# Gram products of an RWKV-7 chunk, parted by key tokens into quadrants

## The chip, the cores and the metric

The kernel runs on one core of a Trainium2 chip. The metric is the device time of the whole program in microseconds (us); lower is better. The core has five engines that run side by side: TensorE (PE in the profile, its weight loads PEld), VectorE (DVE), ScalarE (ACT), GpSimd (POOL) and SyncE (SP, which here issues nearly all DMAs).

## The reference, cut to what matters

One layer of a streaming encoder: RMSNorm, one input projection, two head groups, an output projection. The part that matters is the RWKV-7 recurrence of group A: 16 heads of width 64, in chunks of 64 tokens behind 16 meta tokens.

```python
CHUNK = 64; N_META = 16; SEQ = 512; RWKV_HEAD = 64; N_RWKV_HEADS = 16

def step(S, inp):
    r_t, w_t, k_t, v_t, kk_t, b_t = inp
    sa = jnp.einsum('bhvk,bhk->bhv', S, kk_t)
    S = (S * w_t[:, :, None, :]
         - sa[..., None] * b_t[:, :, None, :]
         + v_t[..., None] * k_t[:, :, None, :])
    y_t = jnp.einsum('bhvk,bhk->bhv', S, r_t)
    return S, y_t
...
hn = _rmsnorm(h_res, norm_in_g[l])
P = hn @ w_in[l]
...
y = _rwkv7_recurrence(rh, decay, kh, vh, kk, kk * ah)
...
bonus = jnp.sum(rh * kh * r_k[l], axis=-1, keepdims=True) * vh
y_a = (yn + bonus.reshape(bsz, L, D_RWKV)) * jax.nn.silu(g_r)
...
h_res = h_res + mix @ w_out[l]
```

The kernel computes a chunk at once instead of token by token. For that it needs, for each chunk and head, the products of two sets of 64 key vectors (b and k, scaled by the decays) with two sets of 64 token vectors (kk and r): a Gram matrix of 128 x 128. Only pairs with the key ahead of the token count, so each of its four 64 x 64 blocks is masked to a triangle.

## The kernel before, in words

The heads go in pairs, 8 in all; a pair fills the 128 partitions, one head on the first 64 and one on the last. The main work is the input projection: 65 column tiles of 128, each against all tokens with TensorE. A tile's weights come in four quarters. SyncE loads two quarters at a time (`wr`), ScalarE rounds a quarter (line 151), VectorE takes the remainder (line 152), and TensorE multiplies the rounded and the remaining parts (lines 352 and 367, `ps_k`, `ps_r`, `ps_v`, `ps_g`, `ps_C`, `ps_h`, `ps_B`, `ps_gc`).

The recurrence's preparation is threaded through this stream. `prepare(i)` handles a pair and calls `fill(ns)` wherever TensorE must not wait for the other engines: `fill` then issues main products worth that many nanoseconds. `until(...)` issues main products until a tile has been taken up. TensorE's order is the order in the program; the other engines' orders are planned from priorities (`ahead()` raises one) and a model of the engines. `later(ns, fn)` issues DMAs once so much main work has gone by, and `behind` issues one behind the last weight load.

The steps of `prepare(i)` that the change touches:

- `bk` holds per chunk the two key sets b and k and, for the second head, b once more (so that the order k, b can be read as one run); `ar` holds the two token sets. Lines 715, 718 and 726 fill `bk`.
- `gt` is the masked Gram tile, 128 rows (two key sets of 64) x 2 heads x 9 chunks x 128 (two token sets of 64); one buffer for even pairs, one for odd ones. Line 750 clears what the meta chunk leaves out.
- `gram` (line 754) issues, for each of 8 chunks and 2 heads, one fp32 product with 64 contracted rows, 128 keys as the stationary side and 128 tokens moving. Chunks 1 to 4 go to two banks `za` (the tag `tz`), chunks 5 to 8 to two banks `zc` (the tags `misc` and `ser`).
- `gram_meta` does the meta chunk and the key norms (line 786) in the next main tile's banks, ahead of the other chunks or behind them (`late`); line 775 masks, line 779 copies the norms.
- `masked` (line 795) multiplies a bank with the mask `gmask` into `gt`, one VectorE instruction for a head and four chunks.
- Lines 817 to 820 form the sums over a head for the bonus term in the bank with tag `ser` and copy them to `r`; line 917 multiplies them with v.
- Line 826 transposes the keys; line 841 stores `gt` (`sg`), line 849 reads it back as 16 x 16 blocks (`d`), lines 859 to 886 invert these on VectorE, line 901 stores the result and `load_inverse` brings it back.

`invert` then works on two pairs together: it builds the inverse of the 64 x 64 blocks from the 16 x 16 ones with small products (lines 961 to 1027). `recur` runs the chunks (lines 1100 to 1139), and the output projection follows (line 1381).

Of the kernel before, what the change touches and what calls it, by code (L numbers as in the profile page):

```python
# [9 lines left out]
F32 = mybir.dt.float32  # L10
# [79 lines left out]
def hymba_kernel(ctx: ExitStack, tc: tile.TileContext, xt, xtok, front, w_in, w_out, pv, lup, cst, msk, gf, out):  # L90
# [533 lines left out]
    def until(*key):  # L624
        while key not in ready:
            step()
# [22 lines left out]
    def c3(t):  # L649
        return t.rearrange("p (c s) -> p c s", s=CH)  # L650

    def lora_up(i):
# [40 lines left out]
    def prepare(i):  # L693
# [3 lines left out]
        ar = cq.tile([P, NCH, 2, CH], F32, tag="ar", name=f"ar{i}")  # L697
        bk = cq.tile([P, NCH, 3, CH], F32, tag="bk", name=f"bk{i}")
        e1 = cq.tile([P, NCH, CH + 1], F32, tag="e1", name=f"e1{i}")
# [15 lines left out]
        nc.vector.scalar_tensor_tensor(  # L715
            out=bk[:, :, 0], in0=c3(k), scalar=hv[:, 2, i : i + 1], in1=c3(te), op0=ALU.mult, op1=ALU.mult
        )
        nc.scalar.copy(bk[64:128, :, 2], bk[64:128, :, 0])
        nc.gpsimd.tensor_scalar(
# [5 lines left out]
        nc.vector.tensor_tensor(out=ta, in0=ta, in1=k, op=ALU.mult)  # L725
        nc.vector.tensor_tensor(out=bk[:, :, 1], in0=c3(ta), in1=c3(e2), op=ALU.mult)
        nc.gpsimd.tensor_copy(dd[:, :, place[i]], e1[:, :, CH])
# [22 lines left out]
        nc.gpsimd.memset(gt[:, :, 0, META:P], 0.0)  # L750

        def gram(z, c, c0):
            for h, hs, ho in heads:
                nc.tensor.matmul(  # L754
                    z[h][:, c - c0],
                    bk[hs, c, h : h + 2, :].rearrange("p a s -> p (a s)"),
                    ar[hs, c].rearrange("p a s -> p (a s)"),
                    start=True, stop=True,
                )

        def gram_meta():
            z = early or next_banks()
            norms = key_norms(z[0][:, 96 : 96 + NS])
            for h, hs, ho in heads:
                nc.tensor.matmul(
                    z[h][:, 0:META],
                    bk[hs, 0, h : h + 2, :].rearrange("p a s -> p (a s)"),
                    ar[hs, 0, 0, 0:META],
                    start=True, stop=True,
                )  # L770
            if p and "levels" in state:
                state["out"] = state.pop("levels").pop(0)(second_level(z))
            with ahead():
                for h in range(2):
                    nc.vector.tensor_tensor(
                        out=gt[:, h, 0, 0:META], in0=z[h][:, 0:META], in1=gmask[:, h, 0:META], op=ALU.mult
                    )
            with ahead():
                nc.scalar.copy(n2, norms)
            if "out" in state:  # L780
                state.pop("out")()
            state["banks"] = z
# [8 lines left out]

        def masked(z, c0, c1):
            with ahead():
                for h in range(2):
                    nc.vector.tensor_tensor(
                        out=gt[:, h, c0:c1],
                        in0=z[h],
                        in1=gmask[:, h].unsqueeze(1).to_broadcast([P, c1 - c0, P]),
                        op=ALU.mult,
                    )  # L800


# [16 lines left out]
        nc.tensor.matmul(zb, ones[:, 0:P], rl, start=False, stop=True)  # L819
        nc.scalar.copy(r, zb)  # L820
        fill(FW["misc"])


        bt = cq.tile([P, 2, NCH - 1, CH], F32, tag="bt", name=f"bt{i}")
        for a in range(2):
            nc.vector.transpose(bt[:, a], bk[:, 0 : NCH - 1, a])

# [76 lines left out]
        for h, hs, ho in heads:  # L904
            for b in range(2):
                for a in range(2):
# [757 lines left out]
```

## Time and profile before

| | |
|---|---|
| median of 3 runs | 993.47 us (991.86 to 994.09) |
| the profiled execution | 993.5 us, span 991.2 us |
| TensorE clock granted | 0.998 |
| busy: TensorE, its loads, VectorE, ScalarE, GpSimd | 99%, 92%, 71%, 39%, 13% |
| DMA | 176.89 MB, mean 178 GB/s |

The span runs from the first instruction to the last. A row of the profile names the line, the engine, the operation and the tiles (written <- read), then the shape; `x32` is the number of records. A form such as `64*128 64x128` at TensorE means 64 rows and 128 columns of the array in use, and 64 partitions x 128 elements moving. Each fp32 product here leaves two records. Matmul durations overlap in the pipeline; what a group costs is seen in the chain, where only the time that each adds is counted.

### The profile page before, as it was taken

The numbers are of one execution on the slowest core, as the hardware profiler recorded it, in microseconds if no ns is written. First come the engines' busy times: TensorE is split into PE (matmuls) and PEld (weight loads), VectorE is DVE, ScalarE is ACT, GpSimd is POOL, SyncE is SP. The second block draws the span as 40 slices with busy tenths as digits, with TensorE's granted clock in tenths as the row PEclk, the third lists the DMA queues.
The fourth block names the chain that finished last, engine by engine and source line by source line (L and its number), as shares of the span: only waits on it lengthen the run. The fifth ranks groups of instructions, "written<-read, shape, count | busy, mean of one in ns | idle before, by whom it ended". The sixth has DMA issues, their size and how long they took to land.

```text
span 991.2 us, 23393 instructions
## 1 busy us (share of the span) xinstructions
PE 981.2 (99%) x9511; PEld 907.4 (92%) x9511; DVE 707.8 (71%) x1413; ACT 390.4 (39%) x731; POOL 128.0 (13%) x242
## 2 busy tenths in 40 slices
PE   9999999999999999999999999999999999999996
PEld 8999999999998999998999998889889898788885
DVE  6777966578675679653779654465756697998897
ACT  7553432344322434322434323232332435546464
POOL 0110302012010121010111010011211102001001
PEclk9999999999999999999999999999999999999999
DMA  9526576246675385853375856988886697697654
GB/s 324 156 91 149 145 202 160 88 126 150 152 181 166 92 194 117 211 150 107 87 186 122 205 143 189 280 250 250 229 252 189 179 281 197 183 313 197 149 128 170
DMA packets 205387, 176.89 MB, mean 178 GB/s; under 512 B 138528, under 2 KB 168032, under 8 KB 204768
## 3 DMA queue, kind: packets, MB, share of 16 engines
q1 hardware_dynamic: 202688, 166.50, 60.2%
q0 software_dynamic: 2304, 8.39, 4.9%
q8 instruction: 74, 1.21, 0.5%
q10 hardware_dynamic: 288, 0.52, 0.1%
q14 instruction: 33, 0.27, 0.1%
HBM read 139.02 MB, written 36.35 MB: 177 GB/s over the span
## 4 chain that ended last, share of the span: by engine, by line
PE 94%; DVE 3%; DMA 1%; ACT 1%; issue 1%; SPq 0%; DVEq 0%; POOL 0%; ACTq 0%
PE ps_v L352 9%; PE ps_h L352 9%; PE ps_C L352 9%; PE ps_g L352 9%; PE ps_gc L367 9%; PE ps_B L367 9%; PE ps_k L352 8%; PE ps_r L352 8%; PE M L1381 5%; PE P L1381 4%; PE Q L1381 2%; PE g L754 2%; PE ps_lora L367 1%; PE ps_k L367 1%; PE zy L1139 1%; PE ps_r L367 1%
## 5 line engine op out<-in xcount | busy, mean ns | idle before, releaser
L151 ACT CAST w<-wr 128x512 fp32r<-128x512 f32 x252 | 153.7, 619 | 285.8 <-PE ps_C L352 47.5
L152 DVE TENSOR_TENSOR w<-wr,w 128x512 fp32r<-128x512 f32 x252 | 175.3, 707 | 117.7 <-ACT w L151 116.7
L352 PE MATMUL ps_v<-xh,w 128*128 128x256 f32 (+2 forms) x512 | 84.0, 285 | 0.0
L367 PE MATMUL ps_B<-xh,w 128*128 128x512 f32 x256 | 83.4, 394 | 0.0
L352 PE MATMUL ps_h<-xh,w 128*128 128x256 f32 (+2 forms) x512 | 81.6, 281 | 0.0
L352 PE MATMUL ps_g<-xh,w 128*128 128x256 f32 (+2 forms) x512 | 81.5, 281 | 0.0
L367 PE MATMUL ps_gc<-xh,w 128*128 128x512 f32 x256 | 81.1, 392 | 0.0
L352 PE MATMUL ps_C<-xh,w 128*128 128x256 f32 (+2 forms) x512 | 80.8, 280 | 0.0
L352 PEld LDWEIGHTS ps_v<-xh,w 128*128 128x128 f32 x512 | 73.9, 188 | 0.3
L352 PE MATMUL ps_k<-xh,w 128*128 128x256 f32 (+1 forms) x448 | 73.4, 285 | 0.0
L352 PE MATMUL ps_r<-xh,w 128*128 128x256 f32 (+1 forms) x448 | 72.6, 281 | 0.0
L352 PEld LDWEIGHTS ps_h<-xh,w 128*128 128x128 f32 x512 | 72.1, 189 | 0.3
L352 PEld LDWEIGHTS ps_g<-xh,w 128*128 128x128 f32 x512 | 72.0, 189 | 0.4
L352 PEld LDWEIGHTS ps_C<-xh,w 128*128 128x128 f32 x512 | 71.7, 189 | 0.2
L352 PEld LDWEIGHTS ps_k<-xh,w 128*128 128x128 f32 x448 | 64.7, 188 | 0.4
L352 PEld LDWEIGHTS ps_r<-xh,w 128*128 128x128 f32 x448 | 63.5, 189 | 0.2
L352 PE MATMUL ps_h<-xl,w 128*128 128x256 f32 x256 | 57.3, 281 | 0.0
L367 PEld LDWEIGHTS ps_gc<-xh,w 128*128 128x128 f32 x256 | 47.8, 188 | 10.0
L367 PEld LDWEIGHTS ps_B<-xh,w 128*128 128x128 f32 x256 | 47.8, 188 | 9.7
L352 PE MATMUL ps_C<-xl,w 128*128 128x256 f32 x256 | 56.2, 280 | 0.0
L352 PE MATMUL ps_v<-xl,w 128*128 128x256 f32 x256 | 55.8, 278 | 0.0
L352 PE MATMUL ps_g<-xl,w 128*128 128x256 f32 x256 | 55.5, 278 | 0.0
(382 smaller groups left out, 2143.6 us busy)
## 6 DMA issues: line engine op xcount, KB each, us to landing
wr<-in_w_in_dram SPq DMA_DIRECT2D x126, 512.0 KB
ct<-opd SPq DMA_DIRECT2D x72, 192.0 KB
wo<-in_w_out_dram SPq DMA_DIRECT2D x24, 512.0 KB
x<-in_w_out_dram POOLq DMA_DIRECT2D x16, 512.0 KB, 5.7
opd<-ar SPq DMA_DIRECT2D x8, 576.0 KB
opd<-gt SPq DMA_DIRECT2D x16, 288.0 KB
bd<-bt SPq DMA_DIRECT2D x64, 64.0 KB
bw<-bd SPq DMA_DIRECT2D x16, 256.0 KB
```

Of the source, the lines that this page charges most:

```text
L151: nc.scalar.copy(hi, rq)
L152: low[q] = eng.tensor_tensor(out=lo, in0=rq, in1=hi.bitcast(F32), op=ALU.subtract).ins
L352: nc.tensor.matmul(ps[r][:, 0 : b - a], ww[:, k * P : (k + 1) * P], xx[:, kt, a:b], start=(kt == 0 and n == 0), stop=(kt == KT - 1 and n = ...
L367: nc.tensor.matmul(ps[r], ww[:, w], xx[:, kt, a:b], start=(kt == 0 and n == 0), stop=(kt == KT - 1 and n == 2))
L754: nc.tensor.matmul(z[h][:, c - c0], bk[hs, c, h : h + 2, :].rearrange("p a s -> p (a s)"), ar[hs, c].rearrange("p a s -> p (a s)"), start= ...
L1139: nc.tensor.matmul(zy[e][hs if e else ho, k], t[hs, o : o + CH], x, start=(n == 0), stop=(n == 2))
L1381: nc.tensor.matmul(bank[s], left(prod, jj, m, s), w, start=(jj == 0 and n == 0), stop=(jj == 7 and n == 2))
```

## The change

The keys are laid out in two halves of 32 tokens each, and each half gets its own products: the first half with all tokens of the chunk, the second half with the last 32 tokens alone (a later key never acts on an earlier token, so the quadrant of last keys with first tokens is zero). A product now has 64 stationary columns (32 keys of two sets). Neighbouring chunks of a bank go to its two halves of partitions: `za` takes the first half of the keys for all 8 chunks, `zc` the second half. The zero quadrants of `gt` are cleared by GpSimd. The masks become 16 VectorE instructions on 32 partitions each; of the first keys with the last 32 tokens nothing has to be masked, only signed, which 12 ScalarE copies do. The bonus sums move behind both fills, and after the transposes and the stores of the Gram tile in the program's order.

```diff
-        bk = cq.tile([P, NCH, 3, CH], F32, tag="bk", name=f"bk{i}")
+        HC = CH // 2
+        bk = cq.tile([P, NCH, 2, 3, HC], F32, tag="bk", name=f"bk{i}")
...
         nc.vector.scalar_tensor_tensor(
-            out=bk[:, :, 0], in0=c3(k), scalar=hv[:, 2, i : i + 1], in1=c3(te), op0=ALU.mult, op1=ALU.mult
+            out=bk[:, :, :, 0], in0=c4(k), scalar=hv[:, 2, i : i + 1], in1=c4(te), op0=ALU.mult, op1=ALU.mult
         )
-        nc.scalar.copy(bk[64:128, :, 2], bk[64:128, :, 0])
+        nc.scalar.copy(bk[64:128, :, :, 2], bk[64:128, :, :, 0])
...
+        g5 = gt.rearrange("p h c (a t) -> p h c a t", a=2)
+        m4 = gmask.rearrange("p h (a t) -> p h a t", a=2)
+        nc.gpsimd.memset(gt.rearrange("p h c (a t) -> p (h c) a t", a=2)[:, :, :, 0:HC], 0.0)
         nc.gpsimd.memset(gt[:, :, 0, META:P], 0.0)
 
-        def gram(z, c, c0):
-            for h, hs, ho in heads:
-                nc.tensor.matmul(
-                    z[h][:, c - c0],
-                    bk[hs, c, h : h + 2, :].rearrange("p a s -> p (a s)"),
-                    ar[hs, c].rearrange("p a s -> p (a s)"),
-                    start=True, stop=True,
-                )
+        def keys(hs, h, c, f):
+            return bk[hs, c, f, h : h + 2].rearrange("p a s -> p (a s)")
+
+        def gram(z, f):
+            for n in range((NCH - 1) // 2):
+                for x in range(2):
+                    c = 2 * n + x + 1
+                    for h, hs, ho in heads:
+                        nc.tensor.matmul(
+                            z[h][64 * x : 64 * x + 64, n], keys(hs, h, c, f),
+                            ar[hs, c, :, HC:CH] if f else ar[hs, c].rearrange("p a s -> p (a s)"),
+                            start=True, stop=True,
+                        )
+
+        def parts_of_rows(h, f):
+            for x in range(2):
+                for a in range(2):
+                    yield x, slice(64 * x + 32 * a, 64 * x + 32 * a + 32), slice(64 * a + 32 * f, 64 * a + 32 * f + 32)
...
-                nc.tensor.matmul(
-                    z[h][:, 0:META],
-                    bk[hs, 0, h : h + 2, :].rearrange("p a s -> p (a s)"),
-                    ar[hs, 0, 0, 0:META],
-                    start=True, stop=True,
-                )
+                nc.tensor.matmul(z[h][0:64, 0:META], keys(hs, h, 0, 0), ar[hs, 0, 0, 0:META], start=True, stop=True)
...
                 for h in range(2):
-                    nc.vector.tensor_tensor(
-                        out=gt[:, h, 0, 0:META], in0=z[h][:, 0:META], in1=gmask[:, h, 0:META], op=ALU.mult
-                    )
+                    for x, src, to in list(parts_of_rows(h, 0))[0:2]:
+                        nc.vector.tensor_tensor(
+                            out=gt[to, h, 0, 0:META], in0=z[h][src, 0:META], in1=gmask[to, h, 0:META], op=ALU.mult
+                        )
...
-        def masked(z, c0, c1):
+        def signed(to, h, c0, zh, a, sign):
+            nc.scalar.activation(g5[to, h, c0:NCH:2, a, HC:CH], zh[:, :, a, HC:CH], AF.Copy, scale=sign)
+
+        def masked(z, f):
+            N = (NCH - 1) // 2
             with ahead():
-                for h in range(2):
-                    nc.vector.tensor_tensor(
-                        out=gt[:, h, c0:c1],
-                        in0=z[h],
-                        in1=gmask[:, h].unsqueeze(1).to_broadcast([P, c1 - c0, P]),
-                        op=ALU.mult,
-                    )
-
+                for h in (1, 0):
+                    for x, src, to in parts_of_rows(h, f):
+                        if f:
+                            nc.vector.tensor_tensor(
+                                out=g5[to, h, 1 + x : NCH : 2, :, HC:CH], in0=z[h][src],
+                                in1=m4[to, h, :, HC:CH].unsqueeze(1).to_broadcast([32, N, 2, HC]), op=ALU.mult,
+                            )
+                        else:
+                            zh = z[h][src].rearrange("p n (a t) -> p n a t", a=2)
+                            nc.vector.tensor_tensor(
+                                out=g5[to, h, 1 + x : NCH : 2, :, 0:HC], in0=zh[:, :, :, 0:HC],
+                                in1=m4[to, h, :, 0:HC].unsqueeze(1).to_broadcast([32, N, 2, HC]), op=ALU.mult,
+                            )
+                            later_part = (to, h, 1 + x, zh)
+                            if to.start // 64 == h:
+                                signed(*later_part, slice(0, 1), -1.0)
+                                signed(*later_part, slice(1, 2), 1.0)
+                            else:
+                                signed(*later_part, slice(0, 2), 1.0)
...
-        zc = [pi.tile([P, 4, P], F32, tag=("misc", "ser")[h], name=f"g{i}_5_{h}") for h in range(2)]
-        for c in range(1, NCH):
-            gram(za if c < 5 else zc, c, (c - 1) // 4 * 4 + 1)
+        zc = [pi.tile([P, 4, 2, HC], F32, tag=("misc", "ser")[h], name=f"g{i}_5_{h}") for h in range(2)]
+        gram(za, 0)
+        gram(zc, 1)
         if not late:
             gram_meta()
-        masked(za, 1, 5)
-        masked(zc, 5, 9)
-        fill(FW["gram2"] - FW["meta"].get(i, 0))
-
-        zb = pi.tile([P, SEQ], F32, tag="ser", name=f"zb{i}")
-        nc.tensor.matmul(zb, ones[:, 0:P], rh, start=True, stop=False)
-        nc.tensor.matmul(zb, ones[:, 0:P], rl, start=False, stop=True)
-        nc.scalar.copy(r, zb)
-        fill(FW["misc"])
+        masked(zc, 1)
+        masked(za, 0)
+        fill(FW["gram2"] + FW["misc"] - FW["meta"].get(i, 0))
...
+        zb = pi.tile([P, SEQ], F32, tag="ser", name=f"zb{i}")
+        nc.tensor.matmul(zb, ones[:, 0:P], rh, start=True, stop=False)
+        nc.tensor.matmul(zb, ones[:, 0:P], rl, start=False, stop=True)
+        nc.scalar.copy(r, zb)
         until("v", i)
```

Lines 726 and 826 read and write `bk` in the new order with the same number of instructions.

More of the change, by code (lines that the diff above doesn't have):

```diff
@@ L650, in c3, with c4 @@
         return t.rearrange("p (c s) -> p c s", s=CH)
+    def c4(t):
+        return t.rearrange("p (c f s) -> p c f s", f=2, s=CH // 2)
     def lora_up(i):
@@ L725, in prepare @@
         nc.vector.tensor_tensor(out=ta, in0=ta, in1=k, op=ALU.mult)
-        nc.vector.tensor_tensor(out=bk[:, :, 1], in0=c3(ta), in1=c3(e2), op=ALU.mult)
+        nc.vector.tensor_tensor(out=bk[:, :, :, 1], in0=c4(ta), in1=c4(e2), op=ALU.mult)
         nc.gpsimd.tensor_copy(dd[:, :, place[i]], e1[:, :, CH])
@@ L807, in prepare @@
         za = [pz.tile([P, 4, P], F32, tag="tz", name=f"g{i}_1_{h}") for h in range(2)]
-        zc = [pi.tile([P, 4, P], F32, tag=("misc", "ser")[h], name=f"g{i}_5_{h}") for h in range(2)]
-        for c in range(1, NCH):
-            gram(za if c < 5 else zc, c, (c - 1) // 4 * 4 + 1)
+        zc = [pi.tile([P, 4, 2, HC], F32, tag=("misc", "ser")[h], name=f"g{i}_5_{h}") for h in range(2)]
+        gram(za, 0)
+        gram(zc, 1)
         if not late:
             gram_meta()
-        masked(za, 1, 5)
-        masked(zc, 5, 9)
-        fill(FW["gram2"] - FW["meta"].get(i, 0))
-        zb = pi.tile([P, SEQ], F32, tag="ser", name=f"zb{i}")
-        nc.tensor.matmul(zb, ones[:, 0:P], rh, start=True, stop=False)
-        nc.tensor.matmul(zb, ones[:, 0:P], rl, start=False, stop=True)
-        nc.scalar.copy(r, zb)
-        fill(FW["misc"])
+        masked(zc, 1)
+        masked(za, 0)
+        fill(FW["gram2"] + FW["misc"] - FW["meta"].get(i, 0))
         bt = cq.tile([P, 2, NCH - 1, CH], F32, tag="bt", name=f"bt{i}")
         for a in range(2):
-            nc.vector.transpose(bt[:, a], bk[:, 0 : NCH - 1, a])
+            nc.vector.transpose(
+                bt[:, a].rearrange("p c (f s) -> p c f s", f=2), bk[:, 0 : NCH - 1, :, a]
+            )
         sg = dp.tile([SCR], F32, tag="sg", name=f"sg{i}")
```

## The prediction

> **What bounds the kernel now.** I read the page first: the span, the busy shares and the chain that ended last.
>
> ```profile
> span 991.2 us, 23393 instructions
> ...
> PE 981.2 (99%) x9511; PEld 907.4 (92%) x9511; DVE 707.8 (71%) x1413; ACT 390.4 (39%) x731; POOL 128.0 (13%) x242
> ...
> PE 94%; DVE 3%; DMA 1%; ACT 1%; issue 1%; SPq 0%; DVEq 0%; POOL 0%; ACTq 0%
> PE ps_v L352 9%; PE ps_h L352 9%; PE ps_C L352 9%; PE ps_g L352 9%; PE ps_gc L367 9%; PE ps_B L367 9%; PE ps_k L352 8%; PE ps_r L352 8%; PE M L1381 5%; PE P L1381 4%; PE Q L1381 2%; PE g L754 2%; PE ps_lora L367 1%; PE ps_k L367 1%; PE zy L1139 1%; PE ps_r L367 1%
> ```
>
> TensorE carries 94% of the chain, and the Gram products (g, L754) are 2% of it. Next come the waits of TensorE alone, longest first:
>
> ```profile
> PE pwarm L202 <- DVE cold L199: 1.0, 1, 1.0
> PE ps_lora L555 <- ACT xh L222: 0.4, 1, 0.4
> PE rz L1100 <- issue: 0.3, 1, 0.3
> PE M L1381 <- DVE o L1350: 0.3, 1, 0.3
> ```
>
> That is the whole list, 2.0 us, and no row of it lies in the Gram part. So a TensorE microsecond saved there is a microsecond of the span, and there is no stall to win back; the other engines matter only if they create one. The profiled execution took 993.5 us, 2.3 us beside its span, and equals the median shown (993.47), so the sum can be made against either.
>
> **The products.** Before, each pair of heads has 16 products (8 chunks, 2 heads), each in two passes, hence 32 records, 256 over 8 pairs. First come their rows by form, then pieces of the chain in order of time (start, length, records).
>
> ```profile
> L754 PE MATMUL g<-ar,bk 64*128 64x128 f32 x256 | 16.4, 278 | 0.0
> L1129 PE MATMUL zs<-uv,bw 128*64 128x64 f32 x256 | 9.2, 225 | 0.0
> L1100 PE MATMUL rz<-st,ct 64*64 64x64 f32 x256 | 8.4, 224 | 0.0
> ...
> 252.57 1.99 PE g L754 x32
> 646.37 1.08 PE zs L1129 x32
> 654.69 1.09 PE rz L1100 x64
> 659.19 0.62 PE rz L1117 x32
> ```
>
> The form says which part of the array a record uses: 64*128 is half its rows and all its columns, 64*64 a quarter. L1100 and L1117 are quarter-array products of the recurrence with 64 moving columns, as the second new product will be. From 32 to 64 records the time grows by 1.09 - 0.62 = 0.47 us, so a record costs 14.7 ns and a group 0.15 us once. With that 0.15 the Gram records cost (1.99 - 0.15)/32 = 57.5 ns, two side by side, and the half-array products of L1129 (64 columns) cost (1.08 - 0.15)/32 = 29.1 ns. So for 64 moving columns a quarter-array record costs half of a half-array one: four run abreast.
>
> After, a pair has 32 products, 64 records, all 64*64: 32 records with 128 moving columns (first half of the keys) and 32 with 64 (second half). The second kind is the row of L1100: 32 x 14.7 = 0.47 us. The first kind is in no row. Its price lies between 14.7 ns (a record as cheap as with 64 columns) and 57.5 ns (no gain from the halved width). I take half of 57.5, 28.8 ns, since L1129 against L1100 shows just that halving: 32 x 28.8 = 0.92 us. So 1.84 us becomes 1.39 us, the 0.15 us stays, and a pair saves 0.45 us: 8 x 0.45 = **3.6 us**. The bounds are 0.90 us a pair (7.2 in all) and a loss of 0.96 (7.7 in all: 32 x 57.5 and 32 x 29.1, less 1.84). The four meta records keep their number with half the width; they take 0.33 us a pair in the chain here:
>
> ```profile
> 254.94 0.33 PE ps_C L765 x4
> ```
>
> I book nothing for them (bounds: 0.08 either way a pair). The two bonus products move behind some main products and cost the same there.
>
> **The masks.** Before, a pair takes 4 VectorE instructions of 128x512 to mask PSUM into the Gram tile. After: 16 of 32 partitions x 256 on VectorE, 12 copies on ScalarE (8 of 128 elements, 4 of 256), 4 instead of 2 small ones for the meta tokens, and a GpSimd memset of 1152 elements a partition. The nearest rows (busy in all, mean of one):
>
> ```profile
> L795 DVE TENSOR_TENSOR gt<-g,cs 128x512 f32<-128x512 f32 x32 | 20.0, 681 | 2.4 <-PE g L754 2.4
> L403 DVE TENSOR_TENSOR hh<-ps_h,rs 128x256 f32<-128x256 f32 x16 | 6.7, 417 | 6.5 <-PE ps_h L352 6.4
> L1016 ACT COPY tm<-ps_k 32x256 f32<-32x256 f32 x8 | 2.9, 364 | 0.1
> L954 POOL MEMSET ts<- 128x512 f32 x8 | 4.0, 524 | 0.0
> L750 POOL MEMSET gt<- 128x224 f32 x8 | 2.3, 285 | 25.1 <-ACT sqx L230 7.4 <-PE ps_k L1005 7.1 <-PE ps_r L1005 6.2
> ```
>
> VectorE: 16 x 0.42 = 6.7 us instead of 4 x 0.625 = 2.5, so 4.2 us more a pair, 34 us in all; I take no discount for the 32 partitions. ScalarE: 8 x 0.28 (the 144-element copy quoted below) + 4 x 0.36 = 3.7 us more a pair. GpSimd: 0.52 + 640 elements x (524 - 285)/288 = 1.06 us. None of it is on the chain if what waits for the masks has room. Who waits: the store of the Gram tile for the inverse (SyncE's in-order queue, weight loads behind it), and VectorE's later work up to the next Gram product.
>
> ```profile
> 122.74 1.88 DVE L795 TENSOR_TENSOR gt<-g,cs 128x512 f32<-128x512 f32 x3
> ...
> 125.22 0.16 DVE L775 TENSOR_TENSOR gt<-ps_C,cs 128x16 f32<-128x16 f32 x1
> 128.96 1.29 SPq L684 DMA_DIRECT2D sg<-gt  x2
> 132.36 0.32 SPq L684 DMA_DIRECT2D d<-sg  x1
> 141.78 0.15 DVE L860 TENSOR_TENSOR tt<-d,nd 72x8 f32<-72x8 f32 x1
> 114.69 0.76 DVE L726 TENSOR_TENSOR bk<-ta,e 128x576 f32<-128x576 f32 x1
> 121.12 1.99 PE g L754 x32
> 100.00:121.00 21.00, 21.00 (x180) 20.91 (x178) 18.63 (x35) 9.08 (x17) 6.92 (x9) 1.00 0.56 136
> ```
>
> In pair 1 the masks run from 122.74 to 125.4, and SyncE reaches the store only at 128.96: 3.6 us of room, and a further stretch until VectorE takes the block up at 141.78 (the load is issued at 132.36). After an even pair the store follows the masks at once, so there SyncE and VectorE fall behind by what the masks lose. The next reader is the odd pair's Gram product: its keys (L726) are done at 115.45 and it starts at 121.12, 5.7 us of room; VectorE is busy 18.63 of the 21 us before it, so 2.4 us of a lag is caught up in this stretch. A lag of 4.2 us fits, and I book nothing for the masks; without that room each microsecond of lag would cost one in each of four odd pairs.
>
> **A new wait.** ScalarE's signed copies read the same PSUM banks as VectorE's masks. How the program orders such a pair shows at the meta tokens, where ScalarE copies other columns of the bank that VectorE reads:
>
> ```profile
> 85.37 0.28 ACT L779 COPY n<-ps_v 128x144 f32<-128x144 f32 x1 [3.23 <-DVE gt L775]
> ...
> ACT n L779 <- DVE gt L775: 20.5, 8, 3.2
> ```
>
> In all 8 pairs the copy waits for VectorE. So each of the 8 first-half masks can make VectorE wait for a ScalarE copy, unless the other head's bank is free meanwhile. Fully in series the masks take 8 x 0.42 + 8 x 0.42 + 3.7 + 4 x 0.16 = 11.1 us, 8.5 more than the 2.6 now; with the two banks alternating, VectorE's own 16 x 0.42 + 4 x 0.16 = 7.4 us, 4.8 more. I take the latter, because VectorE has the other head's bank and the second-half masks to go on with. Queued behind a waiting mask are VectorE's weight splits. The Trainium skill (PSUM — Partial Sum Buffer, section Terms) counts two engines on one bank and quadrant at once as a collision, reads against reads included; the row agrees that they are kept apart.
>
> **The rivals.**
>
> *A, forecast:* the products run four abreast and the masks are covered: 993.5 - 3.6 = 989.9.
>
> *B, the masks in series:* they lag by 8.5 us instead of 4.8. The 5.7 us of room before the odd Gram product, with 2.4 us of catching up, no longer quite holds, and one place has no room at all, weight quarters behind the inverse of pair 3:
>
> ```profile
> 152.83 10.90 PE ps_gc L367 x48
> ...
> 289.44 0.39 PE L367 MATMUL ps_B<-xh,w 128*128 128x512 f32 x1
> 291.68 0.73 ACT L486 ACTIVATE cv<-u,pvt 128x512 f32<-128x512 f32 x1 [10.42 <-POOL u L484]
> ...
> 293.89 0.68 DVE L152 TENSOR_TENSOR w<-wr,w 128x512 fp32r<-128x512 f32 x1
> ```
>
> Such a tile takes 10.90 us, a quarter 2.72, so its third quarter is due at 289.44 + 5.45 = 294.89, and its split ends at 294.57: 0.3 us. An order of VectorE or ScalarE that sets one more instruction ahead of it stalls TensorE. Four odd pairs at 0.5 to 1 us and such a stall of 1 to 2 give 3 to 6 us: 993 to 996. For it: that 0.3 us and the wait row. Against it: the place lies 37 us behind pair 3's masks, and VectorE idles there waiting for TensorE.
>
> *C, slower:* the two column halves don't run abreast with 128 moving columns. The first kind then stays at 57.5 ns, the second at 29.1, and each pair loses 0.96 us: 993.5 + 7.7 = 1001.2. The point from which it loses is 38.3 ns for the first kind, if the second is half of it (32 x 57.5 = 32 x 1.5 x 38.3). It is also the case in which the change doesn't do what it says. Against it: L1100 at 14.7 ns. The Trainium skill (TensorEngine Tiling (Array Packing), section Restrictions) says that column tiling gives up Fast Weight Load, which speaks for C; no row here shows a loss of that sort, since quarter-array records at 14.7 ns bring a weight load each.
>
> *D, slower:* B with a lag that also holds SyncE's weight loads, over 6 us of stalls: 996 to 1000.
>
> **How the numbers follow.** No difference under about 0.2% (2 us) can be told from none. A has 0.57, B 0.25, D 0.10, C 0.08. A is faster by more than that, B within it, C and D slower. The range reaches down to 987.5, where a first-kind record costs 22 instead of 28.8 ns (-1.7) and the meta records shrink by 0.08 us a pair (-0.6), and up to 995.5, which takes in nearly all of B and leaves out C and D. A's own range is 987.5 to 991.5.
>
> **What would show it.** The 64 Gram records of a pair should take about 1.55 us in the chain where 32 took 1.99 (or about 2.95 under C). VectorE's busy time should rise by 26 to 34 us and ScalarE's by about 30, with waits between them at the masks. TensorE's list of waits should stay at about 2 us; under B or D it gains rows released by a weight split (L152), the keys or a Gram mask. I am wrong if the Gram records cost more than 38 ns for the first kind, or if TensorE gains waits of over 2 us.

## The result: slower by 0.75%

| | before | after |
|---|---|---|
| median of 5 runs beside each other | 993.47 us (991.86 to 994.09) | 1000.71 us (996.59 to 1003.69) |
| the profiled execution | 993.5 us, span 991.2 us | 1000.7 us, span 998.9 us |
| ratio | | 1.0075, 95% interval 1.006 to 1.0091 |

The forecast was 989.9 us, in a range of 987.5 to 995.5. The first view again is the page: span, busy shares, and the chain that ended last.

```profile
span 998.9 us, 24144 instructions
PE 980.3 (98%) x9767; PEld 905.2 (91%) x9767; DVE 739.4 (74%) x1525; ACT 413.4 (41%) x827; POOL 135.6 (14%) x250
PE 83%; DVE 7%; DMA 5%; issue 2%; SPq 1%; ACT 1%; DVEq 0%; POOL 0%; ACTq 0%
```

TensorE's busy time is about the same, but the chain that ended last is no longer TensorE's alone: VectorE, DMAs and "issue" have taken 14% of it where they had 5%. TensorE's waits (line, what released it, us in all, times, longest) say where:

```profile
PE t L989 <- DVE xn L974: 4.2, 3, 2.5
PE ps_k L352 <- issue: 1.4, 1, 1.4
PE ps_v L352 <- issue: 1.3, 1, 1.3
PE pwarm L202 <- DVE cold L199: 1.0, 1, 1.0
PE ps_B L367 <- DVE w L152: 0.9, 1, 0.9
PE ps_r L367 <- DVE w L152: 0.5, 1, 0.5
PE ps_gc L367 <- DVE w L152: 0.4, 1, 0.4
PE ps_C L352 <- issue: 0.3, 1, 0.3
PE M L1409 <- DVE o L1378: 0.3, 1, 0.3
```

The list has grown by 8.3 us, from 2.0 to 10.3. Three kinds are new: the products of `invert` (tile `t`) wait for the transposed block `xn` in three of the odd pairs, 4.2 us; main products wait for weight splits, 1.8 us; and main products wait for nothing the profile names ("issue"), 3.0 us. Against the 8.3 us stand the Gram products themselves, in the chain in order of time (start, length, records):

```profile
120.88 1.50 PE g L767 x64
253.64 1.50 PE g L767 x64
```

A pair's 64 records add 1.50 us where 32 added 1.99, as forecast (about 1.55). From the start of one record to that of the next, all Gram products together fell from 15.82 us to 12.04, by 3.8. So 8.3 - 3.8 = 4.5 of the 7.7 us of span are accounted for by this list; the rest is spread over stretches too short for it (other products of the inverse 0.7, `zs` 1.4, some tenths at several main tiles).

**The masks.** The groups by form (busy in all, mean ns of one | idle before, released by):

```profile
L814 DVE TENSOR_TENSOR gt<-g,cs 32x256 f32<-32x256 f32 x64 | 27.0, 421 | 1.5
L820 DVE TENSOR_TENSOR gt<-g,cs 32x256 f32<-32x256 f32 x64 | 26.1, 417 | 5.7 <-ACT gt L806 4.3 <-PE g L767 0.2
L806 ACT ACTIVATE gt<-g 32x128 f32<-32x128 f32 x64 | 13.7, 261 | 24.7 <-DVE gt L820 24.0
L806 ACT ACTIVATE gt<-g 32x256 f32<-32x256 f32 x32 | 12.0, 374 | 17.7 <-DVE gt L820 17.3
L756 POOL MEMSET gt<- 128x1152 f32 x8 | 8.3, 1061 | 27.2 <-ACT sqx L230 9.0 <-PE ps_k L1033 7.1 <-PE ps_r L1033 6.8
```

The prices are the forecast's (0.42 us a mask, 1.06 us the memset, 0.26 and 0.37 us the copies), and VectorE's busy time rose by 31.6 us where 26 to 34 were expected. What the sizes hide is when the masks end. VectorE in time order behind the Gram products of pair 3, which start at 253.6 (start, length, what):

```profile
257.16 0.74 DVE L820 TENSOR_TENSOR gt<-g,cs 32x256 f32<-32x256 f32 x2
257.82 0.67 DVE L152 TENSOR_TENSOR w<-wr,w 128x512 fp32r<-128x512 f32 x1
258.51 0.85 DVE L814 TENSOR_TENSOR gt<-g,cs 32x256 f32<-32x256 f32 x2
...
262.06 0.58 DVE L1065 COPY xT<-ps_C 32x128 f32<-32x128 f32 x2
262.67 0.41 DVE L814 TENSOR_TENSOR gt<-g,cs 32x256 f32<-32x256 f32 x1
263.10 0.28 DVE L1065 COPY xT<-ps_C 32x128 f32<-32x128 f32 x1
...
267.74 0.42 DVE L820 TENSOR_TENSOR gt<-g,cs 32x256 f32<-32x256 f32 x1
268.08 0.67 DVE L152 TENSOR_TENSOR w<-wr,w 128x512 fp32r<-128x512 f32 x1
268.79 0.43 DVE L820 TENSOR_TENSOR gt<-g,cs 32x256 f32<-32x256 f32 x1
```

The small masks are strewn among weight splits (L152), copies of the inverse's second level (L1065, which fall into pairs 3, 5 and 7 only) and short idle stretches. From here on "the lag" is the time from the first Gram record of a pair to the end of the last instruction that writes its block of `gt`. Before, it was 6.5 us in pair 3 and 3.9 in pairs 5 and 7; now it is 16.1, 15.3 and 16.2. In pair 3 the 16.1 us are 7.2 of masks, 7.4 of other work of VectorE (3.7 before) and 1.5 idle. In even pairs it is about 10.5.

**What is late then.** Pair 3's block goes through the inverse on VectorE, out to memory and back, and is transposed for TensorE. Before, this ended just in time (the tile `xn`, then TensorE's products in the chain):

```profile
L946 DVE STREAM_TRANSPOSE xn<-xT x1: 711/711/711, 298.0 to 298.0; 128x512 f32<-128x512 f32 x1
299.82 1.06 PE t L961 x64
```

298.04 + 0.71 = 298.75, so there was 1.1 us of room. After, the chain of this stretch runs through that path:

```profile
293.47 6.08 DMA sx<-y
299.56 0.60 SPq L916
...
300.90 2.96 DMA xT<-sx
303.86 0.02 issue
303.88 0.72 DVE xn L974
304.61 0.14 issue
304.74 0.67 PE t L989 x32
```

The transpose comes 5.8 us later. TensorE, itself 2.4 us later than before, is there 2.5 us before it.

What set the block's store back is not its last mask. SyncE issues its DMAs in order, and in pairs 3, 5 and 7 the store of `gt` (`sg`) stands behind the store of the second level (`opd`), which waits for the copies of L1065. SyncE and VectorE in pair 3 after the change:

```profile
262.67 4.47 SPq L683 DMA_DIRECT2D opd<-xT  x3
...
271.18 1.30 SPq L687 DMA_DIRECT2D sg<-gt  x2
...
274.65 0.33 SPq L687 DMA_DIRECT2D d<-sg  x1
```

```profile
266.24 0.29 DVE L1065 COPY xT<-ps_C 32x128 f32<-32x128 f32 x1
...
279.25 0.16 DVE L402 TENSOR_TENSOR ex<-ps_C,rst 128x4 f32<-128x4 f32 x1 [3.71 <-PE ps_C L352]
279.33 0.15 DVE L884 TENSOR_TENSOR tt<-d,nd 72x8 f32<-72x8 f32 x1
```

Before, the store, the load and the first use of the block stood here:

```profile
266.04 1.31 SPq L684 DMA_DIRECT2D sg<-gt  x2
...
269.44 0.33 SPq L684 DMA_DIRECT2D d<-sg  x1
274.23 0.15 DVE L860 TENSOR_TENSOR tt<-d,nd 72x8 f32<-72x8 f32 x1
```

The last of the second level's copies ends 5.2 us later than before (266.53 against 261.29) and the store comes 5.1 us later. In pairs 5 and 7 the store is issued 14.3 and 15.1 us behind the first Gram record (8.5 before), ahead of the end of the last instruction that writes `gt` (15.3 and 16.2). So on this path the small masks do their harm by pushing those copies back, and the lag only goes along with it.

ScalarE's waits show that the stream of weights is held too (first row before, second after):

```profile
ACT w L151 <- DMA wr<-in_w_in_dram: 19.5, 8, 3.8
ACT w L151 <- DMA wr<-in_w_in_dram: 62.4, 22, 7.0
```

### The profile page after: what moved, and what is told of

Read it like the earlier page. It is cut to its first block, busy times and chain, and to the rows that moved or that the text cites. A ratio compares the mean times of both kernels' runs of the same rounds, so it can differ in the third digit from the quotient of the medians.

```text
span 998.9 us, 24144 instructions
## 1 busy us (share of the span) xinstructions
PE 980.3 (98%) x9767; PEld 905.2 (91%) x9767; DVE 739.4 (74%) x1525; ACT 413.4 (41%) x827; POOL 135.6 (14%) x250
## 4 chain that ended last, share of the span: by engine, by line
PE 83%; DVE 7%; DMA 5%; issue 2%; SPq 1%; ACT 1%; DVEq 0%; POOL 0%; ACTq 0%
PE ps_v L352 9%; PE ps_g L352 9%; PE ps_k L352 8%; PE ps_C L352 8%; PE ps_r L352 8%; PE ps_B L367 7%; PE ps_gc L367 7%; PE ps_h L352 7%; PE M L1409 5%; PE P L1409 4%; DMA wr<-in_w_in_dram 3%; PE Q L1409 2%; PE g L767 1%; DMA in_gt<-in_xt_dram 1%; DVE w L152 1%
## 5 line engine op out<-in xcount | busy, mean ns | idle before, releaser
L152 DVE TENSOR_TENSOR w<-wr,w 128x512 fp32r<-128x512 f32 x252 | 174.2, 707 | 105.1 <-ACT w L151 99.8
L151 ACT CAST w<-wr 128x512 fp32r<-128x512 f32 x252 | 151.5, 618 | 231.3 <-DMA wr<-in_w_in_dram 62.4
```

Source lines behind the costliest of these rows:

```text
L151: nc.scalar.copy(hi, rq)
L152: low[q] = eng.tensor_tensor(out=lo, in0=rq, in1=hi.bitcast(F32), op=ALU.subtract).ins
```

## The experiments

Three theories to start with. **Theory 1**: masks and copies lag, the odd pair's inverse comes late, and TensorE waits for it and for weight splits. **Theory 2**: twice as many small records drain TensorE's supply of instructions ("issue"). **Theory 3**: the moved bonus sums disturb the order. Each version was timed in 5 rounds beside the kernel before. Ratios are to the kernel before, with the 95% interval.

**The parts, each alone, and the change without a part.** e1 issues the signed copies ahead of all masks:

```diff
+        for each head and part: signed(...)     # all 12 copies
         masked(zc, 1)
         masked(za, 0)                           # without its copies
```

> The changed kernel with one edit: the 12 signed ScalarE copies are issued ahead of all masks, so they read the first-half banks while VectorE works on the second-half banks, and the two engines no longer take turns on one bank. Theory 1 (the masks and copies lag, the odd pair's inverse comes late, TensorE waits for it and for weight splits): the masks end some 7 to 8 us after the Gram products instead of 9 to 16, and the time falls from about 1000.5 to 996 to 998. Theory 2 (the doubled count of small TensorE records drains TensorE's instruction supply) and theory 3 (the moved bonus sums disturb the order): unchanged, 999 to 1002.

Measured: 1000.25 us, 1.0068 (1.0055 to 1.008). ScalarE's idle time ahead of its copies falls from 42 us in all to 2, the lag stays at 14.1 to 16.0 in pairs 3, 5 and 7, the time stays. Issuing the copies first doesn't free the masks; e10 and e15 below show that the copies count all the same.

e2 puts the 16 masks, the 12 copies and the memset into the kernel before:

```diff
-        masked(za, 1, 5)
-        masked(zc, 5, 9)
+        for f in (1, 0):                        # half of the keys, 32 partitions
+            masked(za, 1, 5, f)
+            masked(zc, 5, 9, f)
```

> The kernel before with its 64*128 products and its bonus sums in place, and only the masks of the change: 16 VectorE masks of 32x256, 12 signed ScalarE copies and the memset of the zero quadrant for each pair. Theory 1: all of the loss and none of the saving, about 993.5 + 5 = 997 to 1001, with waits of TensorE for the inverse. Theory 2 and theory 3: 993 to 994.

Measured: 994.72 us, 1.0016 (1.0007 to 1.0025). Lag 12.5, 11.6 and 11.7; no wait for `xn`. The same masks cost far less here than in the change.

e3 has the new products and the moved bonus sums with four masks of full width a pair (the blocks then stand in the wrong rows of `gt`, so their placing is left out):

```diff
-        16 masks of 32x256, 12 signed copies
+        4 masks of 128 partitions
```

> The changed kernel with its new products and moved bonus sums, but masked as before: 2 VectorE instructions of 128x512 and 2 of 128x256 for each pair, and no ScalarE copies. The rows of the Gram tile then lie in the wrong places, so this leaves out the right placing of the masked blocks. Theory 1: the waits for the inverse and for weight splits go; what stays is the saving of 3.8 and the stalls of TensorE without a releaser (about 2.7): 991 to 993. Theory 2: those stalls stay, and the time stays above 995. Theory 3: 999 to 1001.

Measured: 991.43 us, 0.9981 (0.9973 to 0.999). The products win, but 1.9 us and not 3.8: two waits at the main products behind the records of pairs 2 and 4 are new, 0.6 us ("issue") and 1.4 us (put down to ScalarE's `sh_v`, L420). e4 is the change with the bonus sums between the two fills again:

```diff
-        fill(FW["gram2"] + FW["misc"] - FW["meta"].get(i, 0))
+        fill(FW["gram2"] - FW["meta"].get(i, 0))
+        (zb: two products, copy to r)
+        fill(FW["misc"])
```

> The changed kernel with the bonus sums put back between the two fills, in the old order. Theory 3: the loss goes, 990 to 994. Theory 1 and theory 2: 999 to 1002, as the changed kernel.

Measured: 995.86 us, 1.0023 (1.0014 to 1.0032), about 5 us better than the change. The lag is the same as in the change (16.3, 15.1, 16.1), but the wait for `xn` falls to 1.7 us and "issue" to 1.2. e8 is the move alone, in the kernel before (the same lines the other way round):

> The kernel before with nothing but the bonus sums moved behind both fills. Theory 3 (the move itself disturbs the order of VectorE and ScalarE): 996 to 998. If it costs only together with the lag of the masks: 993 to 994.

Measured: 994.09 us, 1.0012 (1.0003 to 1.0021), no new wait over 0.2 us. So products with moved sums (e3) and masks (e2) come to -1.9 + 1.6 = -0.3 us, and together they cost 7.5: the loss lies in how they meet.

**Instruction supply.** In the change the stall at pair 2 looks like this in the chain:

```profile
212.14 1.38 PE g L767 x58
213.52 1.35 PE ps_k L352 x10
214.87 1.41 issue
216.28 0.77 PE ps_k L352 x4
```

Nothing that the profile shows releases TensorE there. In the trace's DMA records a 16 KB instruction packet lands at 213.99 + 1.04 = 215.03, 1.25 us before it goes on; at pair 4 and at 742 us the same holds (355.35 + 1.15 and a resume at 357.87; 740.62 + 0.97 and 742.88), and in e3 both waits end 1.4 to 1.5 us behind such a packet, the one put down to ScalarE too. Each time a burst of small records has just gone through (140 at pairs 2 and 4, 128 at 742 us). Such bursts don't always end so: behind the 140 records of pairs 3, 5, 6 and 7 the change shows no such stall. e5 spreads the burst in e3:

```diff
+        fill(2400)          # between the meta group and the Gram products
...
-        fill(FW["gram2"] + ...)
+        fill(FW["gram2"] - 2400 + ...)
```

> The kernel of e3 (new products, 4 VectorE masks for each pair, the right placing of the masked blocks left out), with 2400 ns of main products put between the group of small products of the meta tokens and the Gram products, and taken off the fill behind them. Theory 2 (some 140 small records in a row use up TensorE's instructions faster than they are fetched, and it stands for 0.6 to 1.5 us until the next 16 KB of them have come): the waits without a releaser go, and the time falls from 991.4 to 989.5 to 990. If those waits come from something else: 991 to 992.

Measured: 991.22 us, 0.9982 (0.9973 to 0.9991), no different from e3. "issue" falls from 2.0 to 0.6 us, but the Gram records now save 2.9 instead of 3.8 us, and those of the meta chunk take 0.4 us more: a break between small and main products costs about 0.15 us a pair.

**Later use.** e6 gives the inverse more main work before TensorE takes it up:

```diff
-    solve=24500 ... fill(2 * FW["lev"] - 3000 + FW["out"])
+    solve=29100 ... fill(2 * FW["lev"] - 6000 + FW["out"])
```

> The changed kernel with 4600 ns more main products ahead of the first products with the inverse (L989), of which 3000 are taken off a fill behind them. Theory 1 (the odd pair's inverse comes too late for these products): the wait of L989 for xn, 4.3 us in all, goes, and the time falls from 1000.5 to about 996. Rival (the wait is only where another lateness shows): 999 to 1001, with the wait turning up at another place.

Measured: 1007.63 us, 1.015 (1.0134 to 1.0165): worse. `PE t L989 <- DVE xn L974` is still 5.2 us, and TensorE now waits 5.3 us for VectorE to empty a main tile's banks (u, L403). Both waits for u have one cause in the trace: VectorE stands for 9.8 us at L402, which waits for TensorE's `ps_h` (up to 440.55 and 593.02), and the evacuation of the tile before it (L403, `u`) comes behind that in VectorE's order. e7 joins e4, e5's break and e6:

> The changed kernel with three edits: the bonus sums back between the fills (e4), the small products spread (e5), the first products with the inverse later (e6). If each takes away its own waits: e4's 995.9 less 1.7 (xn) less 1.2 (no releaser) and what late weight splits leave, 991 to 993. If they hand their waits on to each other: 994 to 996.

Measured: 1014.17 us, 1.0214 (1.02 to 1.0228). Waits for u 4.0 us, for `xn` 3.8, and several of 1 to 1.6 us at other places.

**What makes the lag.** Theory 1 now said: VectorE's load. e9 leaves out the masks of the second half of the keys, e10 the copies:

```diff
-        masked(zc, 1)                           # e9
...
-                            signed(...)         # e10: all 12
+        nc.gpsimd.memset(those blocks, 0.0)     # e9 and e10
```

> The change without the 8 VectorE masks per pair of the second half of the keys (their blocks are left at zero by GpSimd, so this part of the Gram tile is left out); products, ScalarE copies and bonus sums as in the change. Theory 1 (VectorE's load in the stretch behind an odd Gram product makes the inverse late): masks on VectorE fall from 7.2 to about 3.8 us a pair, masks end 6 to 11 us behind the Gram product instead of 10 to 16, TensorE's wait for the transpose of xn falls from 4.2 to under 1.5 us: 994 to 996 us. Rival (ScalarE's copies and the banks taken in turns are what costs): they are untouched, so 998 to 1001 us.

Measured: 991.93 us, 0.9986 (0.9977 to 0.9995), better than expected. Lag 11.4, 8.5 and 9.7; no wait for `xn`, none for splits.

> The change without the 12 ScalarE copies per pair (the blocks of first keys with last tokens are left at zero by GpSimd, so this part of the Gram tile is left out); all 16 masks, products and bonus sums as in the change. Theory 1 (VectorE's load): VectorE has the same work, so the time stays near the change's, 997 to 1000 us, with xn and weight splits still among TensorE's waits. Rival (copies and banks in turns): 993 to 996 us, without those waits.

Measured: 993.23 us, 1.001 (1.0001 to 1.0019), as the rival had it. All 16 masks are there, and yet the lag falls to 11.8, 11.3 and 12.6: VectorE's idle time within pair 3's lag falls from 1.5 to 0.4 us and foreign work from 7.4 to 4.1. The copies do count, through the lag. e11 takes load off VectorE elsewhere:

```diff
-    split_w(..., nc.vector)
+    split_w(..., nc.gpsimd if j % 2 and q else nc.vector)
```

> The whole change, with the remainder of every fourth weight quarter formed on GpSimd instead of VectorE: VectorE loses about 65 instructions of 0.68 us (44 us in all, more than the masks added). Theory 1 (VectorE's load): no wait of TensorE for xn or for a split on VectorE is left, 992 to 996 us. Rival (instruction supply and the order carry the loss): 999 to 1002 us. Against both: if GpSimd takes over 3 us for a quarter, TensorE waits for GpSimd and the time is above 1001.

Measured: 1001.5 us, 1.008 (1.0066 to 1.0095). The splits on VectorE take 33.8 us less by sum, but its busy time on the page falls only from 739.4 to 729.8; GpSimd takes 1.53 us a quarter. The lag stays at 16.8, 15.5 and 16.4, and so does the loss. As a test of VectorE's whole load it is weaker than meant, since only 9.6 us went. e12 takes the second level's copies, 2.3 us in each of pairs 3, 5 and 7, from VectorE to ScalarE (on top of e4; busy time 738.8 to 730.6, so no more in all than in e11):

```diff
-    nc.vector.tensor_copy(two[q]["xT"][...], z[e][lo, q])
+    nc.scalar.copy(two[q]["xT"][...], z[e][lo, q])
```

> The change with the bonus sums back between the two fills (995.9 us as it stands), and the copies of the inverse's second level on ScalarE instead of VectorE, which takes 2.3 us of VectorE out of the stretch of the odd pair's masks. Theory 1 (VectorE's load): the odd pair's masks end about 2 us earlier, 993 to 995 us. Rival (VectorE's load is not it): 995 to 997 us.

Measured: 992.09 us, 0.9995 (0.9986 to 1.0004), about 3 us better than e4. Lag 13.9, 12.1 and 13.2; no wait for `xn`. Some 8 us less work at the right place do what 9.6 us less elsewhere did not. These are also the copies that SyncE's store waits for.

That gave **theory L**: what counts is the lag of the odd pair's last mask, whatever makes it. The three parts of it are each measured: the second masks (5 to 7 us), the copies in between (4 us) and the second level's copies (2 to 3 us). e13 puts e12's edit into the whole change, e14 makes the lag without the change, in e2:

```diff
-                        nc.vector.tensor_tensor(out=g5[...], ...)
+                        for _ in range(2 if p and f == 0 else 1):   # e14
+                            nc.vector.tensor_tensor(out=g5[...], ...)
```

> The whole change, bonus sums moved, with only the copies of the inverse's second level on ScalarE instead of VectorE. Theory L (the lag of the odd pair's last mask decides): the lag falls from 15-16 to 12-14 us and TensorE's wait for xn vanishes, 993 to 995.5 us, so most of the 7 us is gone with the bonus sums still moved. Rival (the moved bonus sums are a cause of their own): 996 to 998.5 us, since it differs from the version at 992.1 by the 4.7 us that the move cost in the change.

Measured: 995.54 us, 1.0024 (1.0012 to 1.0036), just above the expectation and below the rival's. Lag 13.7, 12.4 and 12.8, no wait for `xn`; but "issue" is 2.4 us at pair 2 and 1.3 at pair 4, and behind the first the granted clock is 0.5 for 3.4 us, 1.7 us more. So two thirds of the 7.5 us go with these copies alone, and what the moved bonus sums still cost seems to go through the instruction supply: here the packet that ends the stall at pair 2 starts at 214.54, when the burst is over; in e15 below, which has no stall there, at 209.98, before the burst's Gram records.

> The kernel before with its old products and bonus sums in the old place, the small masks and copies of the change, and the 8 masks of the first key half issued twice in odd pairs, which adds 3.5 us of VectorE there and nothing else (the version without the doubling takes 994.7 us, lag 11.6 to 12.5 us, no wait for xn). Theory L: lag of 15 to 16 us, TensorE waits for xn or a weight split in pairs 3 to 7 for 2 to 5 us, 997 to 1000 us. Rival (it takes the new products or the moved bonus sums): 994.5 to 996 us, no such wait.

Measured: 1002.54 us, 1.0093 (1.0075 to 1.0112): by the ratios 7.7 us more than e2 and above the range expected, for 8 extra masks in each of four pairs, with old products and old order. The lag is 15.7, 15.7 and 14.7. But the wait is another than expected:

```profile
PE zb L828 <- DVE xT L1047: 4.5, 3, 1.9
PE zb L828 <- ACT gt L810: 2.5, 2, 2.1
```

Here TensorE stops at the bonus sums (`zb`), which take the bank with tag `ser` that masks and copies read till then (three of the five waits are put down to copies of the second level, which stand between the masks in VectorE's order). There is no wait for `xn`; TensorE has stood still before it. TensorE's waits for masks, copies and weight splits come to 7.0 us against 1.6 in e2; these 5.4 us more and 1.7 us of half clock behind the stall at 130 us make 7.1 of the 7.7 us. In the change the sums come later and don't wait; there the lateness comes out at `xn`.

e15 issues the copies behind all masks, in e12:

```diff
         masked(zc, 1)
         masked(za, 0)                           # without its copies
+        for each head and part: signed(...)     # all 12 copies
```

> The version at 992.1 us (bonus sums back, second level's copies on ScalarE), with the 12 signed copies issued behind all 16 masks instead of between them. If the taking in turns lengthens the lag, VectorE runs its masks through and the last one ends 2 to 3 us earlier (8 us in even pairs, 10 to 11 in odd ones): 990.5 to 992, the weight split waits (1.3 us) gone. If only the number of masks counts: unchanged, 991.5 to 993.

Measured: 990.97 us, 0.9981 (0.9972 to 0.999). This version is 0.19% below the kernel before and the fastest of all that compute the whole result. The time is as expected, a weight split still waits 0.7 us where none was expected, the lag only in part: 9.4 us instead of 10.5 in even pairs, but 13.1, 12.8 and 12.9 in odd ones. Its waits:

```profile
PE ps_v L352 <- issue: 1.1, 1, 1.1
...
PE ps_B L367 <- DVE w L152: 0.7, 1, 0.7
PE zb L849 <- DVE gt L814: 0.4, 1, 0.4
```

e16 is e12 with the break of 2400 ns in pairs 2, 4 and 6 alone:

```diff
+            if early: fill(2400)                # behind gram_meta()
```

> The version at 992.1 us with 2400 ns of main products between the meta group and the Gram products of pairs 2, 4 and 6, so that TensorE's small records come in two bursts there instead of one. If the instruction supply is what is left of the loss: the issue wait of 1.0 us at pair 4 vanishes, at the price of three more changes of mode (0.2 us each): 991.3 to 992. Rival (that wait has another cause): 992 to 993.5, wait unchanged.

Measured: 994.6 us, 1.0019 (1.0008 to 1.0031), worse than e12 and outside both ranges expected. "issue" at pair 4 falls from 1.0 to 0.3 us, so the supply was its cause; but the masks run into other work again (lag 14.7 and 15.1 in pairs 3 and 5), and TensorE waits 1.4 us for L403 and 1.2 for `zb`.

The versions in the order of the lag (mean of pairs 3, 5 and 7). "Store" is when SyncE issues the store of `gt`, from the first Gram record on, mean of the same pairs. Waits, lag and store are those of the profiled executions, which lie up to 2.3 us beside the medians (e10):

| version | lag, us | store, us | TensorE's wait for `xn` | ratio |
|---|---|---|---|---|
| e8, moved sums alone | 4.6 | 10.0 | 0 | 1.0012 |
| e3, products and moved sums, full masks | 4.7 | 10.1 | 0 | 0.9981 |
| before | 4.8 | 10.2 | 0 | 1 |
| e5, e3 with breaks | 6.4 | 8.0 | 0 | 0.9982 |
| e9, second masks out | 9.9 | 11.5 | 0 | 0.9986 |
| e10, copies out | 11.9 | 14.0 | 0.6 | 1.001 |
| e2, masks alone | 11.9 | 13.3 | 0 | 1.0016 |
| e15, e12 with copies last | 12.9 | 13.9 | 0 | 0.9981 |
| e13, the change with level on ScalarE | 12.9 | 13.2 | 0 | 1.0024 |
| e12, level on ScalarE, bonus sums back | 13.1 | 13.6 | 0 | 0.9995 |
| e16, e12 with a break | 13.9 | 14.1 | 0 | 1.0019 |
| e1, copies first | 15.0 | 16.5 | 2.4 | 1.0068 |
| e14, e2 with odd masks twice | 15.3 | 14.3 | 0 (`zb`: 7.0) | 1.0093 |
| e7, sums back, breaks, later use | 15.6 | 12.9 | 3.8 | 1.0214 |
| e4, bonus sums back | 15.8 | 15.6 | 1.7 | 1.0023 |
| the change | 15.9 | 15.7 | 4.2 | 1.0075 |
| e6, later use | 16.1 | 15.7 | 5.2 | 1.015 |
| e11, splits on GpSimd | 16.2 | 15.7 | 2.3 | 1.008 |

Up to 13.9 us of lag, 0.6 us in one version is all the waiting for `xn`; from 15.0 on every version has 1.7 us or more of it, or the 7.0 us at the bank. e4 shows that the lag alone doesn't fix the price. The store parts the versions in the same way (up to 14.3 us, and from 15.6 on), apart from e7, which also moves what comes behind it. Lag and store move together in these runs, so the runs don't separate them. That the store doesn't wait for the last mask is read from the trace.

## Why the prediction was wrong

**The products: right.** 64 records at 1.50 us a pair in the chain (forecast 1.55), 3.8 us in all by record starts (forecast 3.6). The quadrants do run four abreast with 128 moving columns, and rival C is out. Its price had a slip without weight: 32 x 57.5 and 32 x 29.1 ns less 1.84 us is 0.93 us a pair and 7.4 in all, not 0.96 and 7.7. The meta records, booked at nothing within 0.08 us a pair, save 0.11 (0.33 to 0.22 us in pair 3).

**The durations of masks, copies and memset: right.** VectorE 53.1 us of masks instead of 20.0, 31.6 more in all; the copies 25.7 us on ScalarE, whose busy time rose by 23 where about 30 were expected.

**"I book nothing for the masks": the step that failed**, in three places. First the size of the lag: I took it to grow by 4.2 to 4.8 us, the added busy time, and 8.5 in the serial case. In pair 3 it grew by 9.6 us, in pairs 5 and 7 by 11 to 12, because small instructions let other work in between: in pair 3, 7.4 us of foreign work and 1.5 us idle beside the 7.2 us of masks. Second the reader: I looked at the store in pair 1 (3.6 us of room), where no second level is under way. In pairs 3, 5 and 7 the masks push the second level's copies back, and with them SyncE's store of the block, by 5.1 us in pair 3. I also looked at the next odd Gram product (5.7) and a weight quarter (0.3), and left out the reader at the end of the block's own path, where `xn` was ready 1.1 us before TensorE's products. That number stood in the trace of before. Third the cover: behind the store nothing is left, 31.3 us from there to `xn` before, 32.0 after. The "further stretch until VectorE takes the block up", 9.4 us in pair 1, is 4.8 us in pair 3 before (269.44 to 274.23) and 4.7 after (274.65 to 279.33), where VectorE stands 3.7 us at L402, which waits for TensorE and comes first in its order. So 5.8 us arrive where there was room for 1.1.

One stretch of this path stays open. e13 and the change take the block up equally far behind pair 3's first Gram record (25.7 and 25.8 us), and yet e13's `xn` comes 3.8 us earlier: from the issue of `sx<-y` to the loads of the result it needs 2.5 us, the change 6.1, the kernel before 4.3. In the change SyncE also waits 2.9 us for a weight load just there. What sets the time of this transfer isn't shown.

**Rivals B and D** had the mechanism: the weight split at 294.89 with its 0.3 us of room is one of the stalls (`ps_B <- DVE w L152`, 0.9 us, behind pair 3), and weights come later (ScalarE's waits for them 19.5 to 62.4 us). That a lag holds SyncE, as D has it, is what the store shows. D's price of 996 to 1000 comes within 0.7 us of 1000.7, at a chance of 0.10; C's 1001.2 is as near, but by luck, since its products weren't slow. B's argument against itself, that the place lies 37 us behind the masks, was wrong: the inverse carries the lag that far.

**Not foreseen at all: the supply of TensorE's instructions**, as the trace reads: 3.0 us of "issue" in the change and about 2 us of stalls in e3, where it takes half of what the products gain. I counted 32 more records a pair by their 14 to 29 ns on the array and not as instructions to be brought in.

**The moved bonus sums** "cost the same there": alone about 1 us (e8), but 5 us in the change (e4). Once the lag is short, e13 against e12 leaves 3 us, with 2.4 us of "issue" at pair 2 and the slower clock behind it. Versions with the new products in one burst and moved sums show 0.2 to 2.7 us of it there; e4, e12 and e15, with the sums in the old place, none. The packets show that the instructions come later against the burst; why they do, and why so unequally, isn't settled.

Shown by runs: that the small masks and copies are what costs (e3 and e9 against the change), that late masks without the new products and the move can cost as much as the change, though at another wait (e14), and that shortening the lag takes away the wait for `xn` (e9, e12, e13; e10 all but 0.6 us). e11 against e12 speaks for the place of VectorE's work and against its amount, with the reservation above. Only read from the trace: the way from the second level's copies over SyncE's store to `xn`, and that the "issue" stalls are late instruction packets; e5 and e16 agree with the latter, since spreading the records shortens them.

## What to carry to other kernels

Cost an instruction split into many small ones by when the last of them ends and by what it pushes back, not by the sum of their durations: on an engine that is nearly full (VectorE is busy for 14.6 of the 16.1 us in pair 3), other work and turns with a second engine slip in between, here 10 to 12 us for 4.6 us of added work. Read the room in each kind of pair, not in one alone. Follow the result to its last reader and read the room there, however many DMAs and engines lie in between; an order that has just 1 us of room at its end can't pay for a lag anywhere on the path. And when many more TensorE instructions replace fewer, look for waits named "issue" behind the densest burst.

## What the runs showed of the hardware

- A TensorE stream of some 140 small records in a row can be followed by a stall of 0.2 to 2.7 us that no semaphore explains; in the change two of six such streams are. The stalls looked at end 1.2 to 1.5 us behind the end of a 16 KB instruction packet. The Trainium skill (Runtime: NRT & Kernel Launch, section Instruction fetch mechanics) says that an engine streams its instructions in 16 KiB blocks and that this is mostly hidden by the pace at which instructions are issued; at 20 to 30 ns a record it doesn't look hidden here, though no run isolates the fetch.
- Behind a stall the granted clock can fall (e4, e6, e7, e11, e13 and e14 show it). In e4, after 1.7 us of waiting for `xn` and others within 10 us, the windows (last columns: granted clock, DMA share, GB/s) show

```profile
304.00:307.40 3.40, 3.40 (x10) 2.60 (x8) 2.13 (x4) 1.95 (x5) 1.28 (x1) 0.50 0.86 315
307.40:312.00 4.60, 4.60 (x80) 3.65 (x79) 3.73 (x13) 0.97 (x2) 0.00 (x0) 0.99 0.67 215
```

so that a stall can cost 1.7 us more than its own length. The change has stalls of 2.5 us without it, so it doesn't follow from the length alone.
